# Row norms with scaled squares, a biased root and row-scalar operations, and a halved last block, in a hybrid decoder block

## The chip, the cores and the metric

The kernel runs on one core of a Trainium2 chip. The metric is the device time of one launch in microseconds. The core has a matrix engine (PE), whose weight loads are listed apart (PEld), a vector engine (DVE), a scalar engine (ACT), GpSimd (POOL), and queues that start transfers between the chip's main memory and its on-chip memory (most stand on SP). Each engine carries out its instructions in order; semaphores tie the engines together.

## The reference

One decoder layer on a batch of one, with 1024 tokens and 16 meta tokens in front of them, 1024 features, all in float32:

```
rms_norm(x, g) = x * rsqrt(mean(x*x, over features) + 1e-6) * g
h = [meta; x]
xn  = rms_norm(h, g_pre_mix)
mix = merged(gated convolution branch, stick-breaking attention branch)(xn) @ w_out
h   = h + rms_norm(mix, g_post_mix)
u, g = split(rms_norm(h, g_pre_ffn) @ w_up_gate)
ffn = (gelu(causal_dwconv(u)) * g) @ w_down
h   = h + rms_norm(ffn, g_post_ffn);  return h[:, 16:]
```

So each token has four row norms. A row norm is a sum of squares over 1024 features, one inverse root for each token, and a scaling of the row. The change is to these norms.

## The kernel before

Products are made at float32 precision from reduced-precision pieces: each operand is split into a high half (a cast on ACT) and a low half (a subtraction of high from full on DVE or GpSimd), and three matmuls are added up: high by high, high by low, low by high. Several products use a seven-product scheme on 2x2 blocks, with operands named A11, S1, S2, A12, S3, S4, A22 on the weight side and B11, T1, T2, B21, T3, B22, T4 on the token side; the T and S operands are sums and differences, made on DVE.

The stages, in order of time:

1. **Input rows** (lines 301 to 355). Nine blocks of up to 128 rows: square with a row sum on ACT (L327), the inverse root (`rstd_of`, L213), row scaling (L329), transposes on PE, split of the transposed rows (L207, L208). The first products (L277 to L279) are placed among them. This part isn't in a fixed order: the program builder chooses each engine's order by its own estimate.
2. **Input projection, convolution, attention, merge.** About 1110 us; the change doesn't touch it.
3. **w_out and the two norms behind it** (from L1415). Nine blocks of 114 rows, b = 0 to 8. A block has 48 matmuls (L1457 to L1459), in two column halves of 512. Each half is squared with a row sum on ACT (L1469) and multiplied by the gain on DVE (L1474). The two sums are added (L1486); `norm_tasks` (L1394) then gives the scale L1399, the root L1409 and the four operations L1403 to L1406. The row is scaled and added to x (L1490), stored, squared again (L1494), normed again by `norm_tasks`, scaled (L1497), transposed on PE (L1516) and copied into `xr` (L1528). From `xr` the token operands of the up-projection are made: DVE sums (L211), high halves on ACT (L1571), low halves on DVE or GpSimd (L381). Tokens go in two halves, the second of them in three ranges; only the last range needs block 8. The operand T4 of both halves needs memory that comes free when the last block's row scaling is done.
4. **Up-projection, pair 0** (L1628 to L1631): the seven products for the first token half, then for the second. The weight operands of pair 0 and pair 1 are prepared by `pair_tasks` (L1347): casts L1367, low halves on GpSimd (L381), DVE sums.
5. **Up and gate projections, pairs 1 to 21** (L1683 to L1687), each with the preparation of the next pair's weights in between (L1310 on: loads L288, casts L207, low halves on GpSimd L208, sums L1324 and L211), with snapshots of partial sums on ACT (L1692, L1695, L1698), and the convolution and gelu (L257 to L259, L1737).
6. **Down projection** (L1841 to L1843, the last group L1875 to L1877) **and the last norm**, tb = 0 to 7: square with a sum (L1890), the sums L1906 and L1909, root L1912, L1916 to L1919, gain multiply L1896, and the last row operation L1937, after which the rows are stored.

Stages 2 to 4, and the last group of stage 6, are emitted by a planner (`Plan`). Every task has an engine, an estimated cost, tasks that it waits for, and a key. The planner walks through its own simulated time and gives a free engine the ready task with the lowest key; what it emits is then kept in that order on each engine by added dependencies. Tasks for "ANY" go to DVE or GpSimd, whichever is free first. Tasks with `port=True`, all GpSimd tasks and all "ANY" tasks share one slot called port, so that the plan never lets a DVE task of that kind and a GpSimd task overlap; when GpSimd had to wait for the slot, a dependency on the last such DVE instruction is added (`hold`). The small operations of `norm_tasks` are planned without the port. Stages 1 and 5 are ordered by the program builder.

## Time and profile before

| | us |
|---|---|
| median of 3 runs | 1947.39 (1945.9 to 1947.48) |
| the profiled execution | 1943.15 |
| its span, first to last instruction | 1941.0 |
| PE busy | 1898.2 (98%) |
| DVE busy | 1187.0 (61%) |
| ACT busy | 857.3 (44%) |
| GpSimd busy | 554.1 (29%) |

The lists of instructions in order of time that are shown below give: start in us from the span's start, duration in us, engine, line, operation, output and inputs by the program's names, shapes, count. Square brackets give how long the engine was idle before, and what it waited for. In the list of waits, the three numbers are the sum in us, the count, and the longest. In a group, the numbers behind the bar are the busy us and the mean ns of one, and behind the next bar the engine's idle time before it. The granted clock is the share of full speed at which PE ran.

### The profile page before, as it was taken

How to read it: one execution, taken by the hardware profiler on the slowest of the kernel's cores; microseconds unless marked ns; L12 is line 12 of the kernel's file. 1: busy time of each engine (PE TensorE's matmuls, PEld its weight loads, DVE VectorE, ACT ScalarE, POOL GpSimd, SP SyncE). 2: the span in 40 equal slices, each digit the busy share in tenths (PEclk: the TensorE clock that was granted, in tenths of full speed). 3: DMA queues.
4: the chain of work that ended last, by engine and by line, in shares of the span. 5: the costliest groups of instructions: out<-in, count | busy, mean ns of one | idle time of the engine just before them, and what ended most of it. 6: DMA issues, size and time to landing. Idle time of an engine off the chain costs nothing.

```text
span 1941.0 us, 31971 instructions
## 1 busy us (share of the span) xinstructions
PE 1898.2 (98%) x12672; PEld 1764.7 (91%) x12672; DVE 1187.0 (61%) x1803; ACT 857.3 (44%) x1744; POOL 554.1 (29%) x423
## 2 busy tenths in 40 slices
PE   6999999999999999999999999899999999999998
PEld 6999999999999998999989977788899988888887
DVE  6836665656645289999983356845444454355547
ACT  5533433344444367767761234544433444321123
POOL 1110000000000022222333322265565655553351
PEclk9999999999999999999999999999999999999999
DMA  3522112456443687775427763222122221353224
GB/s 143 161 84 88 66 55 77 123 141 169 151 138 103 149 205 210 185 180 153 118 87 225 216 173 104 69 87 87 66 103 72 73 81 66 120 167 104 87 87 141
DMA packets 73841, 238.54 MB, mean 123 GB/s; under 512 B 15400, under 2 KB 17224, under 8 KB 72668
## 3 DMA queue, kind: packets, MB, share of 16 engines
q1 hardware_dynamic: 72396, 233.88, 40.6%
q8 instruction: 99, 1.62, 0.4%
q10 hardware_dynamic: 1296, 2.62, 0.3%
q14 instruction: 50, 0.41, 0.1%
HBM read 166.02 MB, written 70.46 MB: 122 GB/s over the span
## 4 chain that ended last, share of the span: by engine, by line
PE 89%; DVE 6%; ACT 1%; issue 1%; DMA 1%; POOL 1%; SPq 0%; DVEq 0%; POOLq 0%; ACTq 0%
PE st L737 9%; PE st L740 9%; PE st L739 9%; PE st L1683 7%; PE st L1685 7%; PE st L1687 7%; PE mm L277 4%; PE av L974 4%; PE mm L278 3%; PE mm L279 3%; PE st L1843 3%; PE st L1841 3%; PE st L1842 3%; PE tp L955 3%; PE z L915 2%; PE z L916 2%
## 5 line engine op out<-in xcount | busy, mean ns | idle before, releaser
L737 PE MATMUL st<-tT,s_op 128*128 128x260 f32 x864 | 245.3, 284 | 0.0
L740 PE MATMUL st<-tT,s_op 128*128 128x260 f32 x864 | 244.4, 283 | 0.0
L739 PE MATMUL st<-tT,s_op 128*128 128x260 f32 x864 | 244.3, 283 | 0.0
L932 DVE TENSOR_TENSOR_SCAN fl<-fl,upper 114x470 f32<-114x470 f32 (+4 forms) x144 | 206.4, 1455 | 15.8 <-ACT fl L921 15.5
L208 POOL TENSOR_TENSOR a_op<-raw,a_op 128x512 fp32r<-128x512 f32 (+1 forms) x124 | 170.8, 1390 | 66.5 <-ACT a_op L207 63.6
L737 PE MATMUL st<-xnT,s_op 128*128 128x260 f32 x648 | 183.1, 283 | 0.0
L740 PE MATMUL st<-xnT,s_op 128*128 128x260 f32 x648 | 182.9, 282 | 0.0
L739 PE MATMUL st<-xnT,s_op 128*128 128x260 f32 x648 | 182.3, 281 | 0.0
L381 DVE TENSOR_TENSOR s_op<-raw,s_op 128x512 fp32r<-128x512 f32 x157 | 109.4, 698 | 103.0 <-ACT s_op L693 102.7
L693 ACT CAST s_op<-raw 128x512 fp32r<-128x512 f32 x162 | 100.1, 621 | 161.8 <-PE st L740 152.7
L1683 PE MATMUL st<-w_o,a_op 128*128 128x512 f32 (+2 forms) x496 | 162.4, 327 | 2.5 <-ACT snap L1698 1.9
L740 PEld LDWEIGHTS st<-tT,s_op 128*128 128x128 f32 x864 | 163.1, 189 | 0.0
L739 PEld LDWEIGHTS st<-tT,s_op 128*128 128x128 f32 x864 | 162.7, 188 | 0.0
L737 PEld LDWEIGHTS st<-tT,s_op 128*128 128x128 f32 x864 | 162.5, 188 | 0.0
L1685 PE MATMUL st<-w_o,a_op 128*128 128x512 f32 (+2 forms) x496 | 162.3, 327 | 0.0
L1687 PE MATMUL st<-w_o,a_op 128*128 128x512 f32 (+2 forms) x496 | 161.9, 326 | 0.0
L211 DVE TENSOR_TENSOR raw<-raw 128x512 f32<-128x512 f32 x86 | 82.0, 954 | 111.5 <-POOL a_op L208 106.6
L207 ACT CAST a_op<-raw 128x512 fp32r<-128x512 f32 (+1 forms) x124 | 78.0, 635 | 149.7 <-DMA raw<-in_w_up_gate_dram 52.1
L1848 DVE TENSOR_TENSOR acc<-acc,st 128x512 f32<-128x512 f32 x128 | 88.0, 687 | 86.1 <-PE st L1843 86.1
L761 DVE TENSOR_TENSOR su<-st,snap_e 128x260 f32<-128x260 f32 x162 | 69.2, 427 | 91.5 <-PE st L740 87.4
L739 PEld LDWEIGHTS st<-xnT,s_op 128*128 128x128 f32 x648 | 122.1, 188 | 0.0
L737 PEld LDWEIGHTS st<-xnT,s_op 128*128 128x128 f32 x648 | 121.9, 188 | 0.0
(293 smaller groups left out, 5447.2 us busy)
## 6 DMA issues: line engine op xcount, KB each, us to landing
raw<-in_w_in_dram SPq DMA_DIRECT2D x64, 512.0 KB
raw<-in_w_up_gate_dram SPq DMA_DIRECT2D x44, 512.0 KB
act_d<-owork SPq DMA_DIRECT2D x22, 512.0 KB
araw<-act_d SPq DMA_DIRECT2D x22, 512.0 KB
raw<-in_w_down_dram SPq DMA_DIRECT2D x22, 512.0 KB
qh<-qh_d SPq DMA_DIRECT2D x32, 256.5 KB
ql<-ql_d SPq DMA_DIRECT2D x32, 256.5 KB
vv_d<-vt SPq DMA_DIRECT2D x16, 512.0 KB
```

The source lines that it names most:

```text
L208: (lo_engine or nc.vector).tensor_tensor(lo, src, hi.bitcast(F32), op=ALU.subtract)
L211: engine.tensor_tensor(out, a, b, op=ALU.subtract)
L381: eng.tensor_tensor(out, src, hi.bitcast(F32), op=ALU.subtract)
L693: nc.scalar.copy(ops[name][:, 0], src())
L737: nc.tensor.matmul(ps, wt[:, 0, c], xh, start=start and kb == 0, stop=False, skip_group_check=True)
L739: nc.tensor.matmul(ps, wt[:, 0, c], xl, start=False, stop=False, skip_group_check=True)
L740: nc.tensor.matmul(ps, wt[:, 1, c], xh, start=False, stop=kb == 3, skip_group_check=True)
L932: nc.vector.tensor_tensor_scan(fl[:, ::-1], fl[:, ::-1], upper[:, NT - nk:][:, ::-1], 1.0, op0=ALU.mult, op1=ALU.max)
L1683: nc.tensor.matmul(ps, wt[:, 0, k], xh, start=start and kb == 0, stop=False, skip_group_check=True)
L1685: nc.tensor.matmul(ps, wt[:, 0, k], xl, start=False, stop=False, skip_group_check=True)
L1687: nc.tensor.matmul(ps, wt[:, 1, k], xh, start=False, stop=stop and kb == 3, skip_group_check=True)
L1848: nc.vector.tensor_tensor(a, a, ps, op=ALU.add)
```

## The change

Four things are changed.

- **Norms.** The squares are scaled by 1/32 before squaring, so that their sum over 1024 columns is the mean. The root on ACT takes that mean directly, with the epsilon as bias (from a constant tile); where a row's mean comes in parts, the earlier parts and the epsilon are added first, on DVE, and are the root's bias. DVE makes a = -0.5 (mean + eps) in one operation that doesn't wait for the root, then s = 1/root, t = a*s*s, s = (t + 1.5)*s, the last two as tensor_scalar with s as row scalar.
- **Last w_out block** (b = 8). The row addition, the second square and the second scaling go in two column halves, and the first transposes need only the first half. Its keys are 8 lower than before (12 instead of 4 taken off).
- **GpSimd held back** in the plan of stages 3 and 4 (`yields = 10`): GpSimd doesn't take a task that needs the port if a DVE task with the port, of a key lower by more than 10, whose predecessors have all begun, falls due before GpSimd's task would end.
- **The last norm** in the same manner, with the half ahead of the third gain multiply of the last block, and the root's key lower by 1.

```diff
@@ class Plan: add, run
+            unbegun=0, due=0.0)
...
+        def begun(t, end):
+            for u in t.users:
+                u.unbegun -= 1
+                u.due = max(u.due, end + Plan.LAG[t.engine] * (u.engine != t.engine))
+                if u.unbegun == 0 and u.engine == "DVE" and u.port:
+                    soon.append(u)
...
+                        if self.yields and e == "POOL" and t.port:
+                            end = now + (t.cost[e] if t.engine == "ANY" else t.cost)
+                            if any(u.key + self.yields < key and u.due < end for u in soon):
+                                continue
...
@@ norms
-        nc.vector.tensor_scalar(v, ssq, 1.0 / D, EPS, op0=ALU.mult, op1=ALU.add)
-        nc.scalar.activation(s, v, AF.Sqrt)
+    eps = const.tile([P, 1], F32, name="eps")
+    nc.vector.memset(eps, EPS)
+
+    def root(s, last, first=None):
+        nc.scalar.activation(s, last, AF.Sqrt, bias=eps[:last.shape[0]] if first is None else first)
+
+    def half_of(a, last, first=None):
+        if first is None:
+            nc.vector.tensor_scalar(a, last, -0.5, -0.5 * EPS, op0=ALU.mult, op1=ALU.add)
+        else:
+            nc.vector.tensor_scalar(a, last, first, -0.5, op0=ALU.add, op1=ALU.mult)
+
+    def inverse(s, a, t):
         nc.vector.reciprocal(s, s)
-        nc.vector.scalar_tensor_tensor(t, s, v, s, op0=ALU.mult, op1=ALU.mult)
-        nc.vector.tensor_scalar(t, t, -0.5, 1.5, op0=ALU.mult, op1=ALU.add)
-        nc.vector.tensor_tensor(s, s, t, op=ALU.mult)
-        return s
+        nc.vector.tensor_scalar(t, a, s, s, op0=ALU.mult, op1=ALU.mult)
+        nc.vector.tensor_scalar(s, t, 1.5, s, op0=ALU.add, op1=ALU.mult)
...
@@ x_block
-            nc.scalar.activation((xn if b < 2 else junk)[:n], xt[:n], AF.Square, accum_out=ssq[:n])
-            r = rstd_of(small, ssq, n)
+            nc.scalar.activation((xn if b < 2 else junk)[:n], xt[:n], AF.Square, scale=1.0 / 32.0,
+                                 accum_out=ssq[:n])
+            r, a, t = (small.tile([P, 1], F32, name=k, tag=k)[:n] for k in "sat")
+            root(r, ssq[:n])
+            half_of(a, ssq[:n])
+            inverse(r, a, t)
...
@@ norm_tasks
+        ready = (*after, *(plan.add("DVE", 0.15, first, (t,), key) for t in after[:-1]))
+        t = plan.add("ACT", 0.22, rooted, ready, key)
+        a = plan.add("DVE", 0.15, halved, ready, key)
+        return plan.add("DVE", 0.55, newton, (t, a), key), lambda: st["s"]
...
@@ w_out blocks
-            k2 = key + step_o * (c + 1) / 2 - 4
-            t = plan.add("ACT", act_cost(WD) + 0.2, square, (before,), k2, (row,) if c == 0 else ())
-            t = plan.add("DVE", dve_cost(WD) + 0.05, scaled, (t,), k2, (), ("st",))
+            k2 = key + step_o * (c + 1) / 2 - (12 if b == 8 else 4)
+            squares.append(plan.add("ACT", act_cost(WD) + 0.2, square, (before,), k2, (row,) if c == 0 else ()))
+            t = plan.add("DVE", dve_cost(WD) + 0.05, scaled, (squares[-1],), k2, (), ("st",))
...
-        key += step_o - 4
+        key += step_o - (12 if b == 8 else 4)
+        halves = [slice(0, WD), slice(WD, D)] if b == 8 else [slice(0, D)]
...
-        t = plan.add("DVE", 0.15, summed, tuple(rowed), key)
-        t, bst["r"] = norm_tasks(lambda bst=bst: bst["s0"][:QB], QB, key, (t,))
-        t = plan.add("DVE", stt_cost(D), added, (t, x_ld), key, port=True)
+        r_t, bst["r"] = norm_tasks(lambda bst=bst: bst["sums"], QB, key, tuple(squares))
+        adds = [plan.add("DVE", cost, lambda cs=cs, f=added: f(cs), (r_t, x_ld, *rowed), key, port=True) for cs in halves]
...
-            t = plan.add("PE", 0.45, turn, (xv_t,), key + 1, ("st",), turns=True)
+            t = plan.add("PE", 0.45, turn, (xv_ts[-1 if j else 0],), key + 1, ("st",), turns=True)
...
+    plan.yields = 10.0
     plan.run()
...
@@ last norm
+        t = None
+        for i, sq_t in enumerate(squares[:-1]):
+            t = plan.add("DVE", 0.15, lambda i=i, f=first: f(i), (sq_t, t), k2)
+        h = plan.add("DVE", 0.15, halved, (t, squares[-1]), k2)
...
-        t = plan.add("ACT", 0.22, root, (t,), k2)
-        r_done = plan.add("DVE", 0.75, newton, (t,), k2, port=True)
+        t = plan.add("ACT", 0.22, rooted, (t, squares[-1]), k2 - 1)
+        r_done = plan.add("DVE", 0.55, newton, (t, h), k2)
```

More of the change, by code (lines that the diff above doesn't have):

```diff
@@ L51, in add @@
         t = SimpleNamespace(engine=engine, cost=cost, emit=emit, key=key, takes=tuple(takes),
-                            frees=frees, port=port or engine in ("POOL", "ANY"), turns=turns, users=[], left=0, number=len(self.tasks))
+                            frees=frees, port=port or engine in ("POOL", "ANY"), turns=turns, users=[], left=0, number=len(self.tasks),
+                            unbegun=0, due=0.0)
         for d in after:
@@ L121, in run @@
                     free[e] = now + t.cost
+                    if t in soon:
+                        soon.remove(t)
+                    begun(t, now + t.cost)
                     for lag, near in ((0.0, True), (Plan.LAG[e], False)):
@@ L1392, in pair_tasks, with norm_tasks, first, rooted @@
         return {name: v[1] for name, v in kept.items()}, tags
[L1394 removed]
+    def norm_tasks(sums, n, key, after):
         st = {}
[L1397 to L1410 removed]
+        def first():
+            st["f"] = osml.tile([P, 1], F32, name="f", tag="f")[:n]
+            nc.vector.tensor_scalar(st["f"], sums()[:n, 0:1], EPS, None, op0=ALU.add)
+        def rooted():
+            st["s"] = osml.tile([P, 1], F32, name="s", tag="s")[:n]
+            root(st["s"], sums()[:n, len(after) - 1:len(after)], st.get("f"))
+        def halved():
+            st["a"] = osml.tile([P, 1], F32, name="a", tag="a")[:n]
+            half_of(st["a"], sums()[:n, len(after) - 1:len(after)], st.get("f"))
+        def newton():
+            inverse(st["s"], st["a"], osml.tile([P, 1], F32, name="t", tag="t")[:n])
+        ready = (*after, *(plan.add("DVE", 0.15, first, (t,), key) for t in after[:-1]))
+        t = plan.add("ACT", 0.22, rooted, ready, key)
+        a = plan.add("DVE", 0.15, halved, ready, key)
+        return plan.add("DVE", 0.55, newton, (t, a), key), lambda: st["s"]
     def stt_cost(n):
@@ L1481, in block_kernel @@
         plan.join((before,), ("mb",))
-        key += step_o - 4
-        def summed(b=b, bst=bst):
-            bst["s0"] = osml.tile([P, 1], F32, name="s0", tag="s0")
-            nc.vector.reduce_sum(bst["s0"][:QB], bst["sums"][:QB], axis=mybir.AxisListType.X)
-        def added(b=b, bst=bst):
-            h = rows[b][:QB]
-            nc.vector.scalar_tensor_tensor(h, h, bst["r"](), xvs[b % 2][:QB], op0=ALU.mult, op1=ALU.add)
-        def squared(b=b, bst=bst):
-            bst["s2"] = osml.tile([P, 1], F32, name="s2", tag="s2")
-            nc.scalar.activation(xvs[b % 2][:QB], rows[b][:QB], AF.Square, accum_out=bst["s2"][:QB])
@@ L1496, in normed, with added, squared @@
-        def normed(b=b, bst=bst):
-            nc.vector.scalar_tensor_tensor(xvs[b % 2][:QB], rows[b][:QB], bst["r2"](), g_pre2[:QB],
+        key += step_o - (12 if b == 8 else 4)
+        halves = [slice(0, WD), slice(WD, D)] if b == 8 else [slice(0, D)]
+        cost = stt_cost(D // len(halves))
+        def added(cs, b=b, bst=bst):
+            h = rows[b][:QB, cs]
+            nc.vector.scalar_tensor_tensor(h, h, bst["r"](), xvs[b % 2][:QB, cs], op0=ALU.mult, op1=ALU.add)
+        def squared(i, cs, b=b, bst=bst):
+            if i == 0:
+                bst["sums2"] = osml.tile([P, 2], F32, name="sums2", tag="sums2")
+            nc.scalar.activation(xvs[b % 2][:QB, cs], rows[b][:QB, cs], AF.Square, scale=1.0 / 32.0,
+                                 accum_out=bst["sums2"][:QB, i:i + 1])
@@ L1503, in block_kernel @@
+        adds = [plan.add("DVE", cost, lambda cs=cs, f=added: f(cs), (r_t, x_ld, *rowed), key, port=True) for cs in halves]
         stored = plan.add("SP", dma_cost(D), lambda b=b, t0=t0: nc.sync.dma_start(h_d[t0:t0 + QB, :], rows[b][:QB]),
-                          (t,), key + 8)
-        t = plan.add("ACT", act_cost(D) + 0.2, squared, (t,), key)
-        t, bst["r2"] = norm_tasks(lambda bst=bst: bst["s2"][:QB], QB, key, (t,))
-        xv_t = plan.add("DVE", stt_cost(D), normed, (t,), key, port=True)
@@ L1508, in block_kernel @@
-        chain_last.append(xv_t)
-        plan.join((xv_t, stored), (row,))
+                          adds, key + 8)
+        squares = [plan.add("ACT", act_cost(cs.stop - cs.start) + 0.2, lambda i=i, cs=cs, f=squared: f(i, cs), (t,), key)
+                   for i, (t, cs) in enumerate(zip(adds, halves))]
+        r_t, bst["r2"] = norm_tasks(lambda bst=bst: bst["sums2"], QB, key, tuple(squares))
+        xv_ts = [plan.add("DVE", cost, lambda cs=cs, f=normed: f(cs), (r_t,), key, port=True) for cs in halves]
@@ L1510, in block_kernel @@
+        xv_t = xv_ts[-1]
+        chain_last.extend(xv_ts)
+        plan.join((*xv_ts, stored), (row,))
         users = []
```

53 lines of the change are left out of this document (17 added, 36 removed).

## The prediction

> **What bounds the kernel now.** I read the page's busy times first, then the matrix engine's own waits, then busy time by stretches around the waits, then the order of events there.
>
> ```profile
> PE 1898.2 (98%) x12672; PEld 1764.7 (91%) x12672; DVE 1187.0 (61%) x1803; ACT 857.3 (44%) x1744; POOL 554.1 (29%) x423
> ```
> ```profile
> PE tp L239 <- DVE xn L329: 10.8, 2, 9.1
> PE st L1516 <- DVE xv L1497: 4.9, 3, 3.8
> ```
> PE is the bound: 98% of 1941.0 us. Its products don't change, so the change can only touch PE's idle time and its slow-clock time: the start (10.8 us for normalised rows), the transposes of the w_out stage (4.9, of which one wait is 3.8), what follows them, and the tail. The stretches (columns: length, then busy time and instructions of PE, PEld, DVE, ACT, POOL, then the granted clock):
>
> ```profile
> 1243.00:1250.00 7.00, 1.97 (x15) 1.42 (x13) 6.83 (x15) 3.31 (x9) 2.12 (x2) 0.87 0.17 53
> 1250.00:1256.00 6.00, 6.00 (x31) 5.74 (x32) 5.05 (x12) 3.08 (x10) 1.35 (x2) 0.58 0.00 0
> 1256.00:1264.00 8.00, 8.00 (x69) 8.00 (x68) 5.50 (x12) 5.22 (x11) 3.37 (x3) 1.00 0.01 2
> 1264.00:1276.00 12.00, 11.65 (x49) 8.71 (x47) 9.19 (x6) 6.51 (x9) 7.42 (x5) 1.00 0.27 87
> 1276.00:1283.00 7.00, 5.34 (x16) 4.25 (x17) 3.53 (x4) 3.26 (x7) 5.53 (x5) 0.76 0.00 0
> ```
> The **first gap**: PE is idle 5.0 of 7 us from 1243, and then gets a clock of 0.58. At the pace of the next row (69 matmuls in 8.00, 0.116 us each) its 31 matmuls would take 3.6 us, so 2.4 more are lost. The **second gap**, from 1276: 1.7 us idle, and 16 matmuls that at 0.238 each (49 in 11.65) take 3.8 take 5.3: 1.5 lost.
>
> What ends the first gap, in order of time on PE and on DVE:
>
> ```profile
> 1233.59 0.28 PE L1628 MATMUL st<-opB,a_op 128*128 128x258 f32 x1
> 1247.44 1.12 PE L1516 MATMUL st<-ident,xv 114*128 114x114 f32 x8 [3.77 <-DVE xv L1497]
> 1249.83 0.58 PE L1628 MATMUL st<-opB,a_op 128*128 128x256 f32 x1 [1.26 <-ACT opB L1571]
> ```
> ```profile
> 1231.08 1.39 DVE L1404 SCALAR_TENSOR_TENSOR t<-s,v 114x1 f32<-114x1 f32 x1
> 1235.29 0.68 DVE L1474 TENSOR_TENSOR row<-st,g_post 114x512 f32<-114x512 f32 x1
> 1236.15 1.96 DVE L381 TENSOR_TENSOR w_o<-xr,w_o 128x516 fp32r<-128x516 f32 x2
> 1238.22 1.50 DVE L1404 SCALAR_TENSOR_TENSOR t<-s,v 114x1 f32<-114x1 f32 x1
> 1240.14 1.29 DVE L1490 SCALAR_TENSOR_TENSOR row<-row,s,xv 114x1024 f32<-114x1024 f32 x1
> 1244.93 1.14 DVE L1406 TENSOR_TENSOR s<-s,t 114x1 f32<-114x1 f32 x1
> 1246.10 1.28 DVE L1497 SCALAR_TENSOR_TENSOR xv<-row,s,g_pre 114x1024 f32<-114x1024 f32 x1
> 1260.14 1.01 DVE L381 TENSOR_TENSOR opT<-xr,opT 128x232 fp32r<-128x232 f32 x1
> ```
> ```profile
> 1244.65 1.40 POOL L381 TENSOR_TENSOR w_o<-xr,w_o 128x564 fp32r<-128x564 f32 x1
> 1259.60 1.29 POOL L381 TENSOR_TENSOR a_op<-raw,a_op 128x512 fp32r<-128x512 f32 x1 [7.85 <-issue]
> 1267.67 4.43 POOL L381 TENSOR_TENSOR a_op<-raw,a_op 128x512 fp32r<-128x512 f32 x2 [0.69 <-DVE raw L211]
> ```
> The last w_out block's matmuls end at 1233.59. Its chain of two norms then needs until 1247.38, while PE has only the first token half's products to do (until 1243.6). Three one-column operations of that chain, or of block 7's ahead of it, last 1.39, 1.50 and 1.14 us. The last stands beside a GpSimd operation that began at 1244.65. All 18 norms of the stage, grouped (count, busy us, mean ns):
>
> ```profile
> L1404 DVE SCALAR_TENSOR_TENSOR t<-s,v 114x1 f32<-114x1 f32 x18 | 12.9, 719 | 0.6
> L1406 DVE TENSOR_TENSOR s<-s,t 114x1 f32<-114x1 f32 x18 | 5.5, 306 | 0.6
> L1405 DVE TENSOR_SCALAR t<-t 114x1 f32<-114x1 f32 x18 | 2.8, 154 | 0.6
> ```
> The forms that read two tensors average 719 and 306 ns; the form that reads one stays at 154.
>
> The second gap:
>
> ```profile
> 1269.90 20.96 SPq L288 DMA_DIRECT2D raw<-in_w_up_gate_dram  x4
> 1275.48 0.69 DVE L1324 TENSOR_TENSOR tmp_s<-raw 128x512 f32<-128x512 f32 x1 [0.97 <-DMA raw<-in_w_up_gate_dram]
> 1277.02 0.59 ACT L1698 COPY snap<-st 128x512 f32<-128x512 f32 x1
> 1277.66 0.49 PE L1683 MATMUL st<-w_o,a_op 128*128 128x512 f32 x1 [1.93 <-ACT snap L1698]
> ```
> PE's fifth product of pair 1 (1277.66) waits for a snapshot on ACT, which stands behind casts of pair 2's weights; these land at about 1275.4, since their buffers are freed by GpSimd's low halves of pair 1, which run from 1259.60 to 1272.10. GpSimd was idle 7.85 us before, while DVE worked through the low halves of the token operands up to 1261.15. So behind the first gap stands a second limit: DVE's, and then GpSimd's, queue.
>
> **The change part by part.**
>
> *Small operations.* A norm had a scaling (and, in the first norm of a block, a sum), a root on ACT, and four DVE operations. Now the root takes the sum directly with a bias, half of the sum is made beside it, and three operations follow, of which two are tensor_scalar with row scalars. No row shows this form. Its ends are 0.15 us (L1405, one tensor) and the 0.72 that L1404 averages; I take 0.15, since it has one tensor input like L1405. Then the stalls of the 18 norms go (12.9 - 18x0.22 + 5.5 - 18x0.16 = 11.5 us of DVE time; unstalled they last 0.22 and 0.16, as the tail's and start's do). DVE has idle time nearly everywhere in this stage, so most of that is worth nothing; what counts is PE's waits for transposes. The two short ones (4.9 - 3.8 = **1.1 us**) I count as gone.
>
> The Trainium skill, SBUF — State Buffer, section "Who interferes with whom", says that a DVE operation with two SBUF inputs contends with a GpSimd operation that reads SBUF, and that tensor_scalar contends only in its two-port modes. L1404, L1406 against L1405 agree with the first; should the row-scalar form enter such a mode, the rule speaks against this gain, and that is in the fourth case below.
>
> *The last block, ranked first and halved.* From the end of its gain multiply (1235.29 + 0.60 = 1235.9) the chain now lasts to 1247.38, 11.5 us. New, with slots of 0.2 for a small operation and 0.65 for 512 columns (between 0.60 and 0.69, from L1474): half and three operations 0.8; first half added 0.65; two halves squared on ACT 1.4; root and hand-over 0.45; three operations 0.6; two halves normalised 1.3; another hand-over 0.1. That is 5.3, and up to one operation of 0.65 in the way before each norm: 6.0 to 6.6, end near 1242. PE then has work until 1243.6, so the 3.77 us wait and most of the 1.26 behind it go, and the slow clock with them: of 5.0 + 2.4 us I leave 2.0 for waits that remain, so PE could finish the second token half 5.4 us earlier than 1263.8, at 1258.4. What is late next: the token operands' low halves, which now stand behind the chain.
>
> *GpSimd held back.* The plan keeps GpSimd from starting when a DVE task ranked 10 us ahead falls due before it would end. Its low halves then go to DVE.
>
> ```profile
> 1233.60:1261.20 27.60, 25.29 (x51) 0.88 0.06 18
> L381 POOL TENSOR_TENSOR w_o<-xr,w_o 128x564 fp32r<-128x564 f32 (+3 forms) x6 | 7.0, 1170 | 21.9 <-DVE s L1403 14.5 <-ACT w_o L1571 4.4 <-DVE w_o L381 3.1
> ```
> In this stretch DVE (first row: length, busy) is busy 25.3 of 27.6 us: it is the bound here. Off it go the stalls 1.39 - 0.22, 1.50 - 0.22 and 1.14 - 0.16, that is 3.4; about 1.6 of its 2.3 idle us fill up, as casts and PE come less late. Onto it come GpSimd's six operations: between none and all 7.0 us of them, on DVE half as long; I take a third, 1.2. Splitting costs 0.1 and two extra small sums 0.4, and two fewer operations in each norm return as much. Sum: -3.4 - 1.6 + 1.2 = **-3.8 us**. The other end is +3.5 (all moved, no stall gone); the best is 5.4, where PE's own end limits.
>
> So GpSimd's run starts near 1255.8 in place of 1259.60, the weights land 3.8 earlier, and PE's fifth product starts near 1273.9. PE itself would be there at 1258.4 + 4x12x0.238 = 1269.8. The first gap's gain of 5.4 is thus partly given back: the second wait grows from 1.93 to about 4 us and keeps its slow clock. Net **3.8 us**.
>
> ```profile
> 11.63 0.19 ACT L327 ACTIVATION_READ_ACCUMULATOR junk<-xt 128x1 f32 x1
> 13.21 0.14 DVE L218 TENSOR_SCALAR v<-ssq 128x1 f32<-128x1 f32 x1
> 15.24 0.21 ACT L219 ACTIVATE s<-v 128x1 f32<-128x1 f32 x1
> 17.23 1.71 DVE L329 SCALAR_TENSOR_TENSOR xn<-xt,s,gb 128x1024 f32<-128x1024 f32 x1
> 19.09 1.94 PE L239 MATMUL tp<-ident,xn 128*128 128x128 f32 x8 [4.37 <-DVE v L218]
> 34.46 0.42 PE L278 MATMUL mm<-xnT,whi 128*128 128x342 f32 x1 [0.79 <-DVE xnT L208]
> ```
> *The start.* Block 2's sum is there at 11.8, but its scaling waits in DVE's order until 13.21 and the root in ACT's until 15.24, behind two casts. Without the scaling the root can follow its square on the same engine, and DVE can go on at 13.35, so block 2's transposes could start up to 3.2 us earlier than 19.09. If the order of issue stays otherwise, only 0.4 is left (one operation and a hand-over for the first block). Later blocks are fed by a full DVE (PE waits 0.79 even now at 34.46), which saves 0.2 per block. I take **2.0** of 0.4 to 3.2.
>
> ```profile
> 1934.84 0.19 ACT L1890 ACTIVATION_READ_ACCUMULATOR sq<-acc 128x1 f32 x1
> 1935.42 0.16 DVE L1909 TENSOR_TENSOR v<-v,fs 128x1 f32<-128x1 f32 x1
> 1936.68 1.41 DVE L1937 SCALAR_TENSOR_TENSOR acc<-mg,s,hb 128x512 f32<-128x512 f32 x2
> ```
> *The tail.* From the last sum (1935.03) to the last output step (1936.68) is 1.65. The partial sums are made early; left are a hand-over 0.13, the half 0.19, the 256-column gain multiply 0.35 (the root runs beside it) and three slots of 0.2: 1.27. **0.4 us**; nothing covers it.
>
> **Sum.** 2.0 + 1.1 + 3.8 + 0.4 = 7.3 us. The profiled execution took 1943.15 (span 1941.0 and 2.15 around it), which gives 1935.85; the three runs have their median 4.24 higher, at 1947.39, which gives **1940.1**.
>
> **Rivals.** *All given back:* GpSimd's run doesn't start earlier, because DVE's queue isn't shortened; PE stands longer at 1277.66. Then 2.0 + 1.1 + 0.4 = 3.5: 1943.9. For it: DVE's 25.3 of 27.6 us. Against: 3.4 us of that is stall.
>
> *Both gaps close:* the queue is 5.4 shorter, the second wait stays under 2 us and its slow clock (1.5) goes; the start gives 3.2. 5.4 + 1.5 + 3.2 + 1.1 + 0.4 = 11.6: 1935.8; a further 1.9 if the second wait goes too, 1933.9. The Trainium skill, TensorE: Matmul & The Clock Gate, table "Why this matters for your kernels", advises to keep PE's idle gaps under about 3 us. By that rule a second wait under 2 us would cost no clock. The trace disagrees: the wait of 1.93 us is followed by a mean clock of 0.76.
>
> *Orders shift, nothing else:* the chain's place ahead makes PE wait for the first half's low operands instead, and the start keeps its order: 0.4 + 0.4 + about 1: 1945.6.
>
> *Slower:* row-scalar operations stall like L1404, and what GpSimd is held from lands on DVE: 7.0 us of its low halves cost DVE 3.5. It decides once DVE's last low half ends after 1261.15; from there each us moves 1259.60 and 1277.66 alike. 3.5 + 0.5 for the splits - 0.4 at the tail: 1951.0, from 1950 to 1953.
>
> **How the numbers follow.** Forecast 0.45 (its own range 1937 to 1943), all given back 0.17, both close 0.13, orders shift 0.14, slower 0.11. The range reaches from 1933.5 to 1946.8: it leaves out the slower case and the ends of the others. What a measurement can tell from no change is 0.2%, 3.9 us: faster is below 1943.5 (0.44 of the forecast, half of the second case and the whole third: 0.65), slower above 1951.3 (over half of the slower case: 0.07), the same between (0.28).
>
> **What would show it.** Right: the new small operations at 0.15 each without long ones; the transposes of block 8 inside the first half's products, no wait over 1 us there, clock 1.0 from 1243 to 1256; GpSimd's pair-1 run starting 3.8 us earlier relative to the end of the w_out matmuls; a longer wait at the fifth product of pair 1; first products about 2 us earlier than 20.85. Wrong: small operations of 0.5 us and more; DVE's token low halves ending no earlier; new waits behind 1290, where the order isn't pinned.

## The result and the profile after

| | before | after |
|---|---|---|
| median of 6 runs each, us | 1946.64 (1944.04 to 1949.52) | 1934.23 (1930.42 to 1936.4) |
| profiled execution / its span, us | 1943.15 / 1941.0 | 1933.87 / 1931.9 |

The ratio of the timed runs is 0.9936, with a 95% interval of 0.9923 to 0.9949: the change is 12.4 us faster (9.9 to 15.0). Between the two traces the span is 9.1 us shorter.

Milestones in the two traces, us from the span's start. The seventh product of pair 1 is the second one whose token operand is opT; behind it the two traces keep the same pace (655.0 and 654.7 us to the end).

| | before | after | gained so far |
|---|---|---|---|
| first product of stage 1 | 20.85 | 18.91 | 1.9 |
| first w_out matmul | 1126.45 | 1123.01 | 3.4 |
| last w_out matmul | 1233.36 | 1231.35 | 2.0 |
| last row scaling of block 8 ends | 1247.38 | 1239.06 | 8.3 |
| fifth product of pair 1 | 1277.66 | 1269.40 | 8.3 |
| seventh product of pair 1 | 1286.01 | 1277.17 | 8.8 |
| span | 1941.0 | 1931.9 | 9.1 |

Busy times of the kernel after, and PE's largest waits at the places that the change touches, from its page (sum, count, longest):

```profile
PE 1893.5 (98%) x12672; PEld 1759.6 (91%) x12672; DVE 1182.5 (61%) x1783; ACT 861.3 (45%) x1746; POOL 550.0 (28%) x420
...
PE st L1716 <- ACT snap L1731: 3.2, 2, 2.9
PE tp L261 <- DVE a L239: 2.8, 1, 2.8
PE st L1548 <- DVE xv L1528: 1.7, 2, 1.5
```

The wait of 3.77 us for block 8's transposes is gone, one of 1.5 is left at another block, and the snapshot's wait (L1731, the old L1698) has grown from 1.93 to 2.9. The stretches around both gaps (length, then busy us of PE, PEld, DVE, ACT, POOL, then the granted clock):

```profile
1241.00:1248.00 7.00, 6.47 (x51) 5.99 (x50) 7.00 (x19) 4.87 (x14) 1.44 (x1) 1.00 0.00 0
1248.00:1254.00 6.00, 6.00 (x50) 5.76 (x49) 5.44 (x12) 3.38 (x8) 2.20 (x3) 1.00 0.01 3
1262.00:1274.00 12.00, 9.14 (x34) 6.94 (x33) 8.73 (x7) 5.78 (x9) 6.77 (x5) 0.87 0.27 87
1231.60:1253.05 21.45, 20.92 (x168) 20.13 (x167) 20.26 (x50) 17.12 (x40) 6.23 (x5) 1.00 0.07 23
```

In the first gap's place PE is now busy 6.47 of 7 us, at full clock; before it was 1.97 of 7, and then a clock of 0.58. The second gap is there as before. The last row is the stretch from the end of w_out to DVE's last low half of the token operands: 21.45 us instead of 27.60.

Block 8's chain in the kernel after, in order of time on DVE, and the PE and GpSimd instructions behind it:

```profile
1232.65 0.68 DVE L1505 TENSOR_TENSOR row<-st,g_post 114x512 f32<-114x512 f32 x1
...
1233.56 0.27 DVE L245 TENSOR_SCALAR t<-a,s 114x1 f32<-114x1 f32 x1
...
1234.12 1.45 DVE L1519 SCALAR_TENSOR_TENSOR row<-row,s,xv 114x512 f32<-114x512 f32 x2
...
1237.64 1.42 DVE L1528 SCALAR_TENSOR_TENSOR xv<-row,s,g_pre 114x512 f32<-114x512 f32 x2
...
1252.25 0.80 DVE L407 TENSOR_TENSOR opT<-xr,opT 128x232 fp32r<-128x232 f32 x1
```
```profile
1238.78 0.95 PE L1548 MATMUL st<-ident,xv 114*128 114x114 f32 x8
1241.75 0.38 PE L1660 MATMUL st<-opB,a_op 128*128 128x256 f32 x1 [0.43 <-ACT opB L1603]
1269.40 0.50 PE L1716 MATMUL st<-w_o,a_op 128*128 128x512 f32 x1 [2.86 <-ACT snap L1731]
```
```profile
1251.50 1.29 POOL L407 TENSOR_TENSOR a_op<-raw,a_op 128x512 fp32r<-128x512 f32 x1 [2.30 <-issue]
```

From the end of the gain multiply (1233.25) to the last row scaling (1239.06) the chain takes 5.8 us instead of 11.5. The transposes wait for nothing.

The small operations and the two long row operations of the w_out stage, grouped (count, busy us, mean ns):

```profile
L1519 DVE SCALAR_TENSOR_TENSOR row<-row,s,xv 114x1024 f32<-114x1024 f32 (+1 forms) x10 | 19.1, 1915 | 0.3
L1528 DVE SCALAR_TENSOR_TENSOR xv<-row,s,g_pre 114x1024 f32<-114x1024 f32 (+1 forms) x10 | 12.9, 1296 | 0.6
L245 DVE TENSOR_SCALAR t<-a,s 114x1 f32<-114x1 f32 x18 | 4.9, 273 | 0.7
L246 DVE TENSOR_SCALAR s<-t,s 114x1 f32<-114x1 f32 x18 | 3.9, 215 | 0.6
```
```profile
L1490 DVE SCALAR_TENSOR_TENSOR row<-row,s,xv 114x1024 f32<-114x1024 f32 x9 | 11.6, 1285 | 0.3
L1497 DVE SCALAR_TENSOR_TENSOR xv<-row,s,g_pre 114x1024 f32<-114x1024 f32 x9 | 11.6, 1284 | 0.7
```

The second fence is the same two row operations before. The small ones don't stall any more (0.27 and 0.22 us on average), but the row addition does, 1.92 us on average instead of 1.29. One of them, beside the GpSimd operation that it met:

```profile
1162.13 2.98 DVE L1519 SCALAR_TENSOR_TENSOR row<-row,s,xv 114x1024 f32<-114x1024 f32 x1
```
```profile
1161.87 2.15 POOL L407 TENSOR_TENSOR mb<-mraw,mb 128x912 fp32r<-128x912 f32 x1 [3.71 <-ACT mb L1458]
```

It lasts 1.7 us longer than 1.29, and GpSimd's operation ends 1.9 us after its start. Before, at the same place of the program, it was the small L1404 that lasted 1.65 us.

### The profile page after: what moved, and what is told of

The parts are those of the page before. It is cut to its first block, busy times and chain, and to the rows that moved or that the text cites. A ratio compares the mean times of both kernels' runs of the same rounds, so it can differ in the third digit from the quotient of the medians.

```text
span 1931.9 us, 31957 instructions
## 1 busy us (share of the span) xinstructions
PE 1893.5 (98%) x12672; PEld 1759.6 (91%) x12672; DVE 1182.5 (61%) x1783; ACT 861.3 (45%) x1746; POOL 550.0 (28%) x420
## 3 DMA queue, kind: packets, MB, share of 16 engines
q10 hardware_dynamic: 1296, 2.62, 0.4%
## 4 chain that ended last, share of the span: by engine, by line
PE 89%; DVE 5%; DMA 2%; ACT 1%; issue 1%; POOL 1%; SPq 0%; DVEq 0%; ACTq 0%; POOLq 0%
PE st L766 9%; PE st L765 9%; PE st L763 9%; PE st L1716 7%; PE st L1718 7%; PE st L1720 7%; PE mm L299 4%; PE mm L300 4%; PE mm L301 3%; PE av L1000 3%; PE st L1874 3%; PE st L1876 3%; PE st L1875 3%; PE tp L981 3%; PE z L941 2%; PE z L942 2%
## 5 line engine op out<-in xcount | busy, mean ns | idle before, releaser
L225 ACT CAST a_op<-raw 128x512 fp32r<-128x512 f32 (+1 forms) x124 | 77.9, 635 | 150.2 <-DMA raw<-in_w_up_gate_dram 52.9
```

## The experiments

Four quantities tell the kernels apart; all are from one trace each but the ratio. "Chain" is the end of block 8's last row scaling and "seventh" the start of pair 1's seventh product, both counted from the start of the last w_out matmul; "wait" is PE's wait for block 8's transposes. Each ratio is taken against runs of the kernel before that were made together with it, so ratios are compared here and not times.

| kernel | time against before | chain | wait | seventh |
|---|---|---|---|---|
| before | 1 | 14.0 | 3.77 | 52.7 |
| after | 0.9936 (0.9923 to 0.9949) | 7.7 | none | 45.8 |
| norms only | 0.9934 (0.9923 to 0.9946) | 8.5 | none | 45.3 |
| not held back | 0.9941 (0.9928 to 0.9953) | 8.7 | 0.55 | 47.5 |
| last block plain | 0.9941 (0.9929 to 0.9953) | 8.5 | none | 45.5 |
| two-tensor forms | 0.9946 (0.9934 to 0.9958) | 8.4 | none | 46.4 |
| last block only | 1.0000 (0.9991 to 1.0009) | 14.7 | 3.65 | 52.9 |
| direct root, old operations | 0.9973 (0.9963 to 0.9984) | 11.5 | 2.44 | 51.7 |
| old order, new operations | 0.9965 (0.9953 to 0.9978) | 12.4 | 2.62 | 50.9 |
| start only | 0.9982 (0.9973 to 0.9991) | 14.2 | 3.77 | 53.4 |
| after, low halves shared | 0.9914 (0.9900 to 0.9927) | 7.7 | none | 42.3 |
| norms only, low halves shared | 0.9924 (0.9910 to 0.9937) | 8.5 | none | 42.9 |
| before, low halves shared | 0.9977 (0.9968 to 0.9986) | 14.0 | 3.75 | 49.9 |

### The norms alone

```diff
-            k2 = key + step_o * (c + 1) / 2 - (12 if b == 8 else 4)
+            k2 = key + step_o * (c + 1) / 2 - 4
...
-        halves = [slice(0, WD), slice(WD, D)] if b == 8 else [slice(0, D)]
+        halves = [slice(0, D)]
...
-    plan.yields = 10.0
```

> The kernel after, but with block 8 whole and ranked like the other blocks and with GpSimd not held back: only the norms are new. Theory 1 (place): the first gap closes because block 8's chain was moved ahead, not because its operations got shorter. Then this kernel keeps the first gap: PE waits 3 us or more for block 8's transposes, the clock behind it falls below 0.7, and the last product of pair 0 starts about 30 us after the last w_out matmul (before: 30.0; after: 22.9). Only start (2.0) and tail (0.3) are gained: 2 to 4 us faster than before. Theory 2 (norms): the shorter norms close it themselves; the last product of pair 0 starts 24 us or less after w_out and the time is 8 us or more under before.

Measured: 1932.5 us against 1945.0, the whole gain. DVE's order in block 8's chain, and what PE did then:

```profile
1231.02 0.68 DVE L1505 TENSOR_TENSOR row<-st,g_post 114x512 f32<-114x512 f32 x1
...
1232.48 1.32 DVE L1519 SCALAR_TENSOR_TENSOR row<-row,s,xv 114x1024 f32<-114x1024 f32 x1
1233.72 2.50 DVE L407 TENSOR_TENSOR w_o<-xr,w_o 128x516 fp32r<-128x516 f32 x4
...
1236.96 1.28 DVE L1528 SCALAR_TENSOR_TENSOR xv<-row,s,g_pre 114x1024 f32<-114x1024 f32 x1
```
```profile
1239.47 0.94 PE L1548 MATMUL st<-ident,xv 114*128 114x114 f32 x8
1269.24 0.50 PE L1715 MATMUL st<-w_o,a_op 128*128 128x512 f32 x1 [1.91 <-ACT snap L1730]
```

Between the end of the gain multiply (1231.62) and the row addition (1232.48) lie 0.9 us. Before, it was 4.2 (1235.9 to 1240.14): two low halves of 1.96 us in sum had slipped in while the root was made on ACT, and L1404 stalled for 1.3. Now the root runs beside the gain multiply, since it takes the sums directly, and there is no time for anything to slip in. Behind the row addition, while ACT squares the row, low halves still slip in (2.50 us). Theory 1 has fallen; theory 2 stands, though one of its signs was missed: pair 0's last matmul starts 25.4 us after the start of the last w_out matmul (30.4 before, 23.1 in the kernel after), not 24 or less.

### GpSimd not held back

```diff
-    plan.yields = 10.0
```

> The kernel after without the holding back of GpSimd in the plan. Theory 1 (place): holding back is worth at most 1 us; the run of low halves of pair 1 on GpSimd starts about 20 us after the end of w_out as in the kernel after (19.9), and the time is within 2 us of it, 10 to 12 us under before. Theory 3 (holding back): without it GpSimd's operations fall into block 8's chain again, a long operation on DVE of 1 us and more stands in that chain, the transposes of block 8 wait 2 us or more, and 4 us or more of the gain go, so that it is 6 to 8 us under before.

Measured: 1933.5 us, 11.5 under before by the ratio. GpSimd's run of low halves of pair 1 starts at 1251.01, 20.1 us after the last w_out matmul; in the kernel after 20.2. No long operation stands in the chain. By the time, the holding back can't be told from nothing; in this one trace PE's wait at the fifth product is longer, 4.36 us instead of 2.86.

### The last block plain, GpSimd held back

```diff
-            k2 = key + step_o * (c + 1) / 2 - (12 if b == 8 else 4)
+            k2 = key + step_o * (c + 1) / 2 - 4
...
-        halves = [slice(0, WD), slice(WD, D)] if b == 8 else [slice(0, D)]
+        halves = [slice(0, D)]
```

> The kernel after with block 8 whole and ranked like the others, and GpSimd still held back. Theory 1 (place): the first gap is back (wait of 3 us or more for block 8's transposes), last product of pair 0 at 29 us or more after w_out, and 5 to 7 us of the gain are lost: 4 to 7 us under before. Theory 2 (norms): gap closed all the same, time within 2 us of the kernel after. Theory 3 (holding back): GpSimd kept out of the chain is what shortens it; the gap is under 1.5 us and at most 3 us of the gain are lost.

Measured: 1933.4 us, and no wait for block 8's transposes. With the new norms, ranking and halving shorten the chain from 8.5 to 7.7 us, and that isn't seen by PE, which has work until some 9.1 to 10.3 us after the last w_out matmul where it does all of the first token half ahead of the transposes (the transposes' start less their wait: 14.1 - 3.8 before, 11.5 - 2.4 and 12.4 - 2.6 in two runs below).

### Two-tensor forms of the small operations

```diff
-        nc.vector.tensor_scalar(t, a, s, s, op0=ALU.mult, op1=ALU.mult)
-        nc.vector.tensor_scalar(s, t, 1.5, s, op0=ALU.add, op1=ALU.mult)
+        nc.vector.scalar_tensor_tensor(t, s, a, s, op0=ALU.mult, op1=ALU.mult)
+        nc.vector.scalar_tensor_tensor(s, t, 1.5, s, op0=ALU.add, op1=ALU.mult)
```

> The kernel after, with the last two small operations of the norms of the w_out stage as operations of two tensor inputs (t = s*a*s and s = (t+1.5)*s) in place of those with row scalars; everything else, count and order included, stays. Theory 4 (the stall only moved): GpSimd makes DVE wait once, at the first operation that it contends with; in the kernel after that is the long row addition (mean 1.92 us, 1.29 before). With two-tensor forms the small operations stall again (mean 0.5 us or more of the 18 t), the row additions fall back to about 1.3 us, DVE's sum over these operations stays within 2 us, and the time within 1.5 us of the kernel after. Rival (removed): the row-scalar forms really take the stall away; then the small operations grow by some 8 us in sum, the row additions stay at 1.9, block 8's transposes are later and the time is 2 us or more above the kernel after. The Trainium skill, SBUF — State Buffer, section 'Who interferes with whom', names two-input operations as those that contend with GpSimd, which fits both.

Measured: 1934.4 us. The stall is partly back on the small operation:

```profile
L1522 DVE SCALAR_TENSOR_TENSOR row<-row,s,xv 114x1024 f32<-114x1024 f32 (+1 forms) x10 | 17.1, 1721 | 0.3
L1438 DVE SCALAR_TENSOR_TENSOR t<-s,a 114x1 f32<-114x1 f32 x18 | 7.1, 395 | 0.6
```

The t operation grew by 2.2 us in sum, the row additions fell by 2.0: in these two traces what DVE loses to GpSimd stays, only the operation that bears it changes. The sizes were smaller than theory 4 said (0.40 us on average, not 0.5), its direction and the unchanged time were right. Which form the small operations have is worth nothing here by itself, since this chain (8.4 us) stays inside PE's work too.

### The last block only, old norms

```diff
-            k2 = key + step_o * (c + 1) / 2 - 4
+            k2 = key + step_o * (c + 1) / 2 - (12 if b == 8 else 4)
...
+        halves = [slice(0, WD), slice(WD, D)] if b == 8 else [slice(0, D)]
...
+        if b == 8:
+            squares = [plan.add("DVE", 0.15, summed2, squares, key)]
```

> The kernel before with the last w_out block ranked first and halved (its two halves of squares are added up by one more small operation), and nothing else: old norms, GpSimd not held back. Theory 1 (place), the prediction's step: the chain of block 8 ends 4 us or more earlier than 13.9 us after the last w_out matmul, the first gap closes by more than half and the time is 4 to 6 us under before. Theory 5 (either closes it): the gap has two cures that don't add up, this one and the norms; the same result, 4 to 6 us, and the pair together no more than the norms alone, which gave 12.5. Theory 2 (norms): with the old operations the stalls and the low halves that slip in stay in the chain; gap under half closed, time within 2.5 us of before.

Measured: ratio 1.0000. In DVE's chain, and on PE:

```profile
1238.45 1.96 DVE L381 TENSOR_TENSOR w_o<-xr,w_o 128x516 fp32r<-128x516 f32 x2
...
1240.52 1.49 DVE L1404 SCALAR_TENSOR_TENSOR t<-s,v 114x1 f32<-114x1 f32 x1
...
1247.83 1.07 DVE L1406 TENSOR_TENSOR s<-s,t 114x1 f32<-114x1 f32 x1
```
```profile
1249.74 1.39 PE L1528 MATMUL st<-ident,xv 114*128 114x114 f32 x8 [3.65 <-DVE xv L1505]
```

The same two low halves slip in, and the same operations stall as before. A rank decides between operations that are ready; while the chain waits for its root on ACT it has none that is ready, and DVE takes the next in rank. So 8 us of rank bought nothing, and the halving added its 0.7 us of extra operations.

### Direct root with the old operations; old order with the new ones

First, the root takes the sums, but the four old operations follow; second, the root waits for gain multiply, sum and half as before, and the three new operations follow.

```diff
@@ direct root, old operations
-            inverse(st["s"], st["a"], osml.tile([P, 1], F32, name="t", tag="t")[:n])
+            nc.vector.reciprocal(s, s)
+            nc.vector.scalar_tensor_tensor(t, s, v, s, op0=ALU.mult, op1=ALU.mult)
+            nc.vector.tensor_scalar(t, t, -0.5, 1.5, op0=ALU.mult, op1=ALU.add)
+            nc.vector.tensor_tensor(s, s, t, op=ALU.mult)
@@ old order, new operations
+        t = plan.add("DVE", 0.15, summed, tuple(rowed), key)
+        t = plan.add("DVE", 0.15, halved, after, key)
+        t = plan.add("ACT", 0.22, lambda: nc.scalar.activation(st["s"], st["a"], AF.Sqrt, scale=-2.0), (t,), key)
```

> Norms only (as in the run of the norms alone), but in the w_out stage with the four old operations behind the root; the root still takes the sums directly, and mean + eps is made beside it. Theory 2a (what the root waits for): the chain got shorter because the root no longer waits for the gain multiply, the sum and the scaling, so no low halves slip in between; then the chain ends about 10.5 us after the last w_out matmul (8.4 with the new operations, 13.9 before), PE's wait for block 8's transposes is under 1 us and the time within 2 us of norms alone. Theory 2b (stalls): the shorter and unstalled operations did it; then L1404-like stalls of over 1 us stand in block 8's chain, it ends 12 us or more after, PE waits 2 us or more and 4 us or more of the gain go.

> Norms only, but in the w_out stage with the old order of steps ahead of the root: gain multiply, then the two sums added, then half, then the root; behind it the three new operations. Theory 2a (what the root waits for): chain ends 11.5 us or more after the last w_out matmul, PE waits over 1.5 us for block 8's transposes, and 3 us or more of the gain go. Theory 2b (stalls): chain ends at 10 us or less, PE waits under 1 us, and the time is within 2 us of norms alone.

Measured: 5.3 us (3.1 to 7.2) and 6.8 us (4.3 to 9.1) under before, by the ratios. Rows of the first on DVE and PE, then of the second, then the stretch behind the second's wait:

```profile
1240.86 1.14 DVE L1442 TENSOR_TENSOR s<-s,t 114x1 f32<-114x1 f32 x1
...
1243.38 0.81 PE L1554 MATMUL st<-ident,xv 114*128 114x114 f32 x6 [2.44 <-DVE xv L1534]
...
1270.90 0.79 PE L1721 MATMUL st<-w_o,a_op 128*128 128x512 f32 x1 [4.27 <-ACT snap L1730]
```
```profile
1231.34 1.81 DVE L407 TENSOR_TENSOR w_o<-xr,w_o 128x516 fp32r<-128x516 f32 x2
...
1239.26 2.27 DVE L1519 SCALAR_TENSOR_TENSOR xv<-row,s,g_pre 114x1024 f32<-114x1024 f32 x1
...
1241.58 1.78 PE L1544 MATMUL st<-ident,xv 114*128 114x114 f32 x8 [2.62 <-DVE xv L1519]
```
```profile
1241.58:1245.58 4.00, 3.07 (x12) 2.51 (x13) 3.79 (x10) 3.66 (x8) 0.77 (x2) 0.50 0.01 2
```

Each half of the norm change shortens the chain (14.0 to 11.5 and to 12.4), and both together to 8.5. Each alone leaves it beyond the end of PE's work, so a wait of 2.4 to 2.6 us stays, with a slow clock behind it (0.50 over 4 us in the last row). Both together pass below that, and wait and slow clock go: the seventh product stands at 51.7 and 50.9 with one half, at 45.3 with both. Only a part of these 6.4 and 5.7 us is lost in the first gap: pair 0's last matmul starts 2.8 and 3.3 us later than with both. The rest is lost in the second gap, by a wait of 4.27 us in the third product of pair 1 and one of 1.96 at the fifth, with slow clocks behind them; GpSimd's run starts at 24.2 and 24.4 there, at 20.5 with both. Neither 2a nor 2b is right alone.

### The start only

```diff
-            nc.scalar.activation((xn if b < 2 else junk)[:n], xt[:n], AF.Square, accum_out=ssq[:n])
-            r = rstd_of(small, ssq, n)
+            nc.scalar.activation((xn if b < 2 else junk)[:n], xt[:n], AF.Square, scale=1.0 / 32.0,
+                                 accum_out=ssq[:n])
+            r, a, t = (small.tile([P, 1], F32, name=k, tag=k)[:n] for k in "sat")
+            root(r, ssq[:n])
+            half_of(a, ssq[:n])
+            inverse(r, a, t)
```

> The kernel before with the new norm in the input rows alone. The prediction's step: 2.0 us of 0.4 to 3.2. First product near 18.9 us instead of 20.9 and the time 2 us under before, w_out's first matmul some 2 us earlier. Rival: the head start is lost in the 1110 us between (a transfer or another engine sets the pace there), w_out's first matmul within 0.7 us of 1126.45 and the time within 1 us of before. A third: the 1.3 us that the kernel after gained on top between its first product and w_out belongs to this part, then 3.3 us in all.

Measured: 3.5 us (1.7 to 5.2) under before. The first product starts at 19.05, 1.8 us earlier. The first w_out matmul stands at 1125.21; over all traces it is between 1124.98 and 1128.65 in the four with the old start (mean 1126.4) and between 1122.35 and 1125.74 in the ten with the new one (mean 1124.1). So the head start arrives, and the 1.5 us that the trace of after has on top is within what the 1100 us between vary from trace to trace. The trace of before has a slow clock there, 0.50 for 3.41 us from 1005.84, which costs 1.7 us; the trace of after has none, nine others have one of 3.41 or 6.83 us near 1000.

### The kernel before once more

No edit.

> The kernel before once more, unchanged, for a second trace of it. Its timed runs spread over 8 us (1941.8 to 1950.1), those of the kernel after over 6, and its first trace was of a run 3.5 us under its median. Theory 6 (waits near 2 us): PE's wait at the fifth product of pair 1 (1.93 us) and at block 1's transposes (0.98) stand near the length from which the granted clock falls; in the first trace the one of 1.93 us slowed the clock (0.50 for some 3 us), in other kernels' traces two of four waits of 1.91 to 1.96 did. Then this trace has the same waits within 0.1 us and differs in where the clock falls. Rival: the spread comes from the 1110 us ahead of w_out (first w_out matmul between 1125 and 1129 in kernels with the old start); then the waits and clocks are alike and the difference stands ahead of 1126.

Measured: 1944.28 us, span 1942.1. The wait at the fifth product is 1.93 us again, and the clock falls behind it in both traces (0.81, 0.50, 0.84 in steps of 2 us, then 0.80, 0.50, 0.85), so theory 6 is wrong there. The first w_out matmul stands 1.1 us earlier than in the first trace (the slow clock at 1005.84 is missing), so the rival isn't enough either. What differs behind it is block 1:

```profile
1148.86 1.28 DVE L1378 TENSOR_TENSOR tmp_s<-raw 128x512 f32<-128x512 f32 x1 [2.23 <-DMA raw<-in_w_up_gate_dram]
...
1161.66 1.00 PE L1516 MATMUL st<-ident,xv 114*128 114x114 f32 x8 [2.77 <-DVE xv L1497]
```

The sum of two weight blocks stands ahead of block 1's norms in DVE's order and waits for its load, which landed late in this execution; PE's wait for block 1's transposes is then 2.77 us instead of 0.98. In the start-only kernel it was 2.46, in the kernel after 1.48, in norms only none.

### Low halves of pair 1's weights shared with DVE

The same edit on the kernel after, on norms only, and on the kernel before; it moves six, five and five of the seven low halves to DVE.

```diff
-            return h, plan.add("POOL", pool_cost(512),
-                               lambda: low(nc.gpsimd, got[name][:, 1], src(), got[name][:, 0]), (h,), key + 1)
+            if i == 1:
+                return h, plan.add("ANY", any_cost(512), made, (h,), key + 1)
+            return h, plan.add("POOL", pool_cost(512), lambda: made("POOL"), (h,), key + 1)
```

> The kernel after, with the low halves of pair 1's weights planned for DVE or GpSimd, whichever is free (six of seven go to DVE, 0.68 us each in place of 1.29). Theory 7 (GpSimd's run sets the second gap): the buffers of the weights come free some 3 us earlier, the loads of pair 2 are issued near 1259 in place of 1261.8, PE's wait at the fifth product falls from 2.86 to under 1 us and its slow clock goes: 3 to 5 us under the kernel after, 15 to 17 under before. Rival (the gelu sets it): ACT's queue has the gelu of pair 0 ahead of that snapshot, which waits for DVE's convolution (3.26 us idle for it in the kernel after); DVE gets 4 us of new work ahead of the convolution, so the wait stays at 2.5 us or more and the time within 1.5 us of the kernel after, or above it.

> The norms alone, with pair 1's low halves shared in the same way (five of seven go to DVE). Theory 7: PE's waits at the third and fifth product of pair 1 (1.08 and 1.91) fall under 0.5 in sum, and the time is 2 to 3 us under the norms alone (15 under before); the clock was not slowed there, so nothing more. Rival (gelu): the waits stay within 0.5 us of these and the time within 1.5 us of the norms alone.

> The kernel before with pair 1's low halves shared between DVE and GpSimd (five of seven go to DVE), and nothing else. Theory 7 holds by itself: GpSimd's run of 12.5 us becomes one of some 7 on both engines, the loads of pair 2 are issued 4 us earlier relative to the last w_out matmul (before 36.5), PE's wait of 1.93 at the fifth product goes with its slow clock (1.5): 2 to 4 us under before. Rival (DVE has no room there): DVE is full until 1261.15, and the new work delays the token halves' last low halves, on which pair 0 waits; PE's wait moves ahead to pair 0's products or to pair 1's first ones, and the time is within 1.5 us of before or above it. Then the second gap could only be cured once the norms had shortened DVE's queue.

Measured: 1928.4, 1930.2 and 1939.75 us; on the kernel before 4.5 us (2.7 to 6.2) under it, which is the only one of the three that was timed beside the kernel it edits. In the first of the three:

```profile
1255.82 17.56 SPq L310 DMA_DIRECT2D raw<-in_w_up_gate_dram  x3
...
1264.31 0.50 PE L1720 MATMUL st<-w_o,a_op 128*128 128x512 f32 x1 [0.54 <-ACT snap L1735]
```

The loads of pair 2 are issued 26.5 us after the last w_out matmul instead of 30.4, PE's wait at the fifth product is 0.54 instead of 2.86 and the clock stays at 1.00 there. The seventh product comes 3.6, 2.4 and 2.8 us earlier than without the edit. Theory 7 holds in all three traces, on the kernel before too: GpSimd's run sets the second gap, and DVE has the room. The next limit shows behind it: PE's wait at the seventh product, which is for DVE (snap, L1760), is 1.81 us in the first instead of 0.32. By the ratios the first is 4.3 us under the kernel after and the second 1.9 under norms only; the intervals (0.9900 to 0.9927 and 0.9923 to 0.9949; 0.9910 to 0.9937 and 0.9923 to 0.9946) come from different comparisons with before and overlap, the second pair by far.

## Why the prediction was right, and where not

**The time** came out inside the range, 5.9 us under the forecast of 1940.1, and nearest to the case in which both gaps close (1935.8). But only one gap closed.

**The step that failed is the first gap's cure.** The prediction gave the last block's rank and halves the whole of it ("end near 1242", "PE could finish the second token half 5.4 us earlier") and the norms' shorter operations 1.1 us, because "DVE has idle time nearly everywhere in this stage". The chain's length was right: 5.8 us (6.6 in norms only), 6.0 to 6.6 forecast. Its cause was not: rank and halves alone gave 1.0000 (0.9991 to 1.0009), the norms alone 0.9934. The time could not show this, as the four parts were changed together: that it lies in the range doesn't speak for this step. It was right that the stalls are worthless where DVE has room; it was overlooked that in block 8's own chain they, and the low halves that slip in while the root is waited for, are the chain.

**Small operations at 0.15.** They take 0.27 and 0.22 (L245, L246). Of the 11.5 us of stalls most were not removed but moved: L1404, L1405 and L1406 had 21.2 us, the operations in their place (L245, L246) have 8.8, but the two row operations grew from 23.2 to 32.0. The rule of the Trainium skill that the prediction weighed (SBUF — State Buffer, "Who interferes with whom") agrees with these rows: the row-scalar form didn't stall (0.28 us at the longest). It was a rule on which operation meets GpSimd, not on whether DVE's time is lost.

**The two short waits, 1.1 us gone.** One of 1.48 us is still there in the trace of after. It goes with the late load at block 1, as in the second trace of before: the sum of two weight blocks waits 2.78 us for its load there, and 1.07 in norms only, where PE doesn't wait, although the row addition behind it stalls in both (2.40 and 2.17 us).

**DVE's queue and GpSimd's start, 3.8 us.** 6.1 in the traces (27.60 to 21.45 us; GpSimd's run starts 20.2 us after the last w_out matmul instead of 26.2). Of its terms, the stalls were read wrongly: 3.4 us were taken off, but the row of 1.39 us begins at 1231.08, ahead of the stretch from 1233.60. What stalls inside it is 2.4 us (1.50 - 0.22, 0.39 - 0.22, 1.14 - 0.16), and the norm operations there fell by 2.5, from 7.6 to 5.1 us (gain multiplies included, overlaps counted once). Idle time fell by 1.1, from 2.3 to 1.2, where 1.6 was forecast. The mis-sized term is GpSimd's work on DVE, taken as 1.2 us more; DVE had some 2.9 us less of token operands to do there (16.4 before, 13.5 after). That fits block 7's chain, which ended sooner (its transposes start 4.1 us ahead of the last w_out matmul instead of 1.7 behind it), so that part of them was done ahead; no run tests this alone.

**The second gap.** Right: the wait grew, to 2.86 where about 4 was forecast, and kept a slow clock (0.87 over 12 us). That it is GpSimd's run which holds it was argued in the prediction, and is shown by the shared low halves.

**The start, 2.0.** 1.9 us in the traces. The root of block 2 did go early:

```profile
11.81 0.30 ACT L235 ACTIVATE s<-ssq,eps 128x1 f32<-128x1 f32 x1
...
15.61 1.40 DVE L355 SCALAR_TENSOR_TENSOR xn<-xt,s,gb 128x1024 f32<-128x1024 f32 x1
17.15 1.94 PE L261 MATMUL tp<-ident,xn 128*128 128x128 f32 x8 [2.81 <-DVE a L239]
```

The full 3.2 wasn't reached since the row scaling was placed behind two low halves of the blocks before it, at 15.61.

**The tail, 0.4.** 0.2: the last sum is there at 1926.13, the last output step starts 1.46 us later (1.65 before).

```profile
1927.25 0.42 DVE L1929 TENSOR_TENSOR mg<-acc,g_post 128x256 f32<-128x256 f32 x1
1927.59 1.41 DVE L1966 SCALAR_TENSOR_TENSOR acc<-mg,s,hb 128x512 f32<-128x512 f32 x2
```

The plan put the gain multiply behind the three small operations; the prediction had it first, with the root beside it.

**The sum.** In the traces 1.9 (start) + 6.8 (seventh product from 52.65 to 45.82 behind w_out) + 0.2 (tail) = 8.9 of 9.1; the w_out stage itself and the 1100 us ahead of it differ by -1.4 and +1.5 and cancel. The +1.5 goes with the slow clock at 1005.84 in the trace of before (1.7 us), which that kernel's second trace doesn't have. The -1.4 belongs to the 6.8: PE does block 7's transposes (0.95 us) inside the w_out stage now, and waits 0.5 us longer at block 1. So some 7.5 of the 9.1 us are the change's, near the 7.3 of the forecast's sum; as the first gap's cure and two terms of the queue were wrong there, that is in part luck. The timed gain of 12.4 has 9.9 at its lower end; the first trace of before was of a run 3.5 us under that kernel's median, so a part of the difference may lie in what a run of before varies by, and the rest stays open.

## What to carry to other kernels

A chain that hops between engines isn't shortened by ranking it first: whatever is ready slips in while it waits for the other engine, so let the hop start earlier (here the root takes the sums, not what is made from them). A chain that runs behind other work costs what it is longer than that work, and the slow clock behind the wait; once it is shorter, more shortening is worth nothing (8.5 and 7.7 us gave the same time). Before counting a stall as removed, look which operation bears it next; and after a gap closes, ask what sets the next one, since sharing seven low halves between two engines was worth a third as much as the whole change (4.5 us on the kernel before, against 12.4).

## What was not expected of the hardware

**A wait of about 2 us sometimes slows the clock and sometimes doesn't.** The granted clock in the 4 us behind a wait of 2.77 us (block 1, second trace of before) and behind one of 2.46 (the same place in the start-only kernel):

```profile
1161.66:1165.66 4.00, 4.00 (x22) 3.30 (x23) 1.20 (x5) 2.73 (x6) 0.65 (x1) 1.00 0.26 96
```
```profile
1161.32:1165.32 4.00, 4.00 (x17) 3.16 (x18) 0.99 (x4) 2.71 (x6) 0.41 (x1) 0.66 0.27 85
```

From the w_out stage on, over the traces, of seven waits between 1.91 and 1.96 us three were followed by a clock near 0.5, of nine between 2.4 and 2.9 us eight, and of 28 between 0.9 and 1.81 that stood by themselves none. So the length alone doesn't decide.

What else decides is where the wait falls. Within a trace the granted clock changes only at times that lie whole steps of 3.413 us apart (in before at 1005.84, 1009.25, 1248.18, 1255.01, 1278.90 and 1282.32, which is 1, 71, 73, 80 and 81 steps after the first), and where the steps lie differs from trace to trace. From the w_out stage on, every step at full clock in which PE was idle for 1.90 us or more in sum was followed by one at 0.50, and no step with 1.82 us or less was (near 1000 us two with 1.6 and 1.7 were, so the bound isn't sharp by these records). Two steps of before, the first with the wait of 1.93 us at the fifth product, then two of norms only, between which its wait of 1.91 us is divided:

```profile
1275.49:1278.90 3.41, 1.49 (x7) 1.05 (x6) 3.21 (x3) 2.12 (x5) 2.71 (x2) 1.00 0.00 0
1278.90:1282.32 3.42, 3.42 (x9) 2.65 (x8) 0.81 (x1) 1.66 (x3) 2.15 (x3) 0.50 0.00 0
```
```profile
1264.92:1268.33 3.41, 2.41 (x11) 1.58 (x9) 1.29 (x2) 1.89 (x4) 1.29 (x1) 1.00 0.34 133
1268.33:1271.75 3.42, 2.51 (x11) 2.05 (x12) 2.17 (x2) 2.48 (x5) 2.98 (x3) 1.00 0.00 0
```

In the first, PE is idle 1.9 of 3.41 us and the next step runs at 0.50; in norms only it is idle 1.0 and 0.9, and the clock stays. The Trainium skill (TensorE: Matmul & The Clock Gate, table in "Why this matters for your kernels") puts the length to stay under at about 3 us; these rows have slow clocks from 1.93 us on. The wait of 2.77 us above was divided in the same way. A slow step costs 1.7 us, and for waits of about 2 to 2.8 us it comes or not by where the steps happen to lie in that execution.
